# One decoder layer, 256 tokens, one core: the rotary queries and the middle norm's first columns transposed by 32x32 squares and transfers

## The chip, the cores and the metric

The kernel runs on one core of a Trainium2 chip. The metric is the time of one execution in device microseconds (us), the median of several runs; lower is better. TensorE (PE) does the matrix products and the 128x128 transposes, VectorE (DVE), ScalarE (ACT) and GpSimd (POOL) the elementwise work, SyncE (SP) issues most transfers (DMAs) between HBM and the on-chip memory.

## The reference

```
h  = x + 1/2 * SwiGLU_1(RMSNorm(x))                 # 1024 -> 2816 -> 1024
u  = RMSNorm(h)
[q_a,k_a,v_a | q_b,k_b,v_b | g_a,g_b] = u @ W_in    # 1024 -> 5120
y_a = block-sparse attention(rotary(q_a), rotary(k_a), v_a)   # 8 heads of 64; 256 tokens are one block
y_b = stick-breaking attention(q_b, k_b, v_b)                 # 8 heads of 64
m  = sigmoid(g_a) * (y_a @ W_branch_a) + sigmoid(g_b) * (y_b @ W_branch_b)   # 512 -> 1024, twice
h  = h + m @ W_out                                  # 1024 -> 1024
h  = h + 1/2 * SwiGLU_2(RMSNorm(h))
out = RMSNorm_final(h)                              # all float32, x is (1, 256, 1024)
```

## The kernel before

The 256 tokens are two halves t = 0, 1 of 128 partitions. Every weight matrix is cut into 376 tiles of 128x512 and laid in one stream in the order in which they are used. `Weights` loads the stream from HBM in chunks of two tiles (`raw`, 512 KB, issued by SP, three buffers), ACT rounds a tile to its high part `wh`, DVE forms the rest `wl`, and each product is three TensorE passes (`mm3`: wh with the high part of the left operand, wl with the high part, wh with the low part; 128x512 each). A *unit* is one such product of one tile and one t; after each unit the program's clock (`weave.tick`) goes on by one and tasks that are due are written into the program there: the delays D_... are counted in units. What stands in an engine's queue runs in that order.

A left operand must have its columns on the partitions, so it is transposed first. There are two ways. `Normed.half` transposes four 128x128 blocks on TensorE into PSUM (`tp_`), then splits them (ACT casts the high part, DVE subtracts). `Normed.moved` transposes 32x32 squares on DVE (one instruction for 128x512), moves the squares with 16 DMAs of 32 partitions from SBUF to SBUF (`exchange`), and splits what landed. Before the change `moved` serves the first 512 columns of the norms u (ahead of the input projection) and z (ahead of the second FFN), and `exchange` serves q and k of the stick-breaking heads; q and k of the rotary heads (`qa`, `ka`; 8 TensorE transposes each, tiles `qtpa`, `ktpa`, ended in qTha/qTla and kTha/kTla) and all four halves of the merged branches m (`tp_m`, `mh`, `ml`; t = 0, 1 and column halves c = 0, 1) go through TensorE.

Where the text speaks of them: input projection `in0`..`in9` (16 units each; `in0` is q of the rotary heads, `in1` its k); POOL rotates qa and ka (four small operations each, `rotate`) after its Newton steps for the scale r_u (`inv_rms`); branch products `ba` (y_a, tiles yah, yal) and `bb` (y_b, ybh, ybl); their gates (`gate`, sigmoids on ACT); `wo` is the product with W_out.

Of the kernel before, what the change touches and what calls it, by code (L numbers as in the profile page):

```python
# [17 lines left out]
P = 128  # L18
# [10 lines left out]
CH = 2  # L29
# [12 lines left out]
D_PIECE = 2  # L42
D_TURN = 10
D_READY = 7
D_NORM = 4
D_SQUARES = 3
D_EIGHT = 6
D_MERGE = 8
D_FIRST = (9, 10)
D_RMS0 = 4  # L50
D_RMS1 = 5
# [77 lines left out]
class Weights:  # L129
# [9 lines left out]
    def load(self, n, tiles=0):  # L139

        n = min(n, N_TILES // CH)
        while self.loaded < n * CH + tiles:
            c, j = divmod(self.loaded, CH)
            if j == 0:
                nm = f"raw{c}"
                self.raw[c] = self.early(nm) if c < 12 else self.pool.tile([P, CH * 512], F32, name=nm, tag="raw", bufs=3)
            step = 1 if c < 4 else CH
            s = slice(j * 512, (j + step) * 512)
            self.nc.sync.dma_start(self.raw[c][:, s], self.stream[c, :, s])
            self.loaded += step  # L150

    def split(self):
        i = self.ready
        self.load(i // CH + 1)
        raw = self.raw[i // CH][:, i % CH * 512:i % CH * 512 + 512]
        hi = self.pool.tile([P, 512], F32R, name=f"wh{i}", tag="wh", bufs=self.bufs)
        lo = self.pool.tile([P, 512], F32R, name=f"wl{i}", tag="wl", bufs=self.bufs)
        g = self.gain(i)
        if g is None:
            self.nc.scalar.copy(hi, raw)  # L160
            self.nc.vector.tensor_sub(lo, raw, hi.bitcast(F32))  # L161
        else:
            self.nc.scalar.activation(hi, raw, AF.Copy, scale=g)  # L163
            self.nc.vector.scalar_tensor_tensor(lo, raw, g, hi.bitcast(F32), op0=ALU.mult, op1=ALU.subtract)  # L164
        self.parts[i] = hi, lo
        self.ready += 1
        if i % CH == CH - 1:
            del self.raw[i // CH]
            self.load(i // CH + 1 + 3)

    def pump(self):
        if self.ready < min(self.freed + self.bufs, self.at + self.ahead, N_TILES):
# [16 lines left out]
def hybrid_layer_kernel(ctx, tc, x, xt, pos, g_final, bgate, wstream, out):  # L189
# [4 lines left out]
    ordered.enter_context(tc.manual_schedule())  # L194
    consts = ctx.enter_context(tc.tile_pool(name="consts", bufs=1))
    wpool = ctx.enter_context(tc.tile_pool(name="wpool", bufs=1))
    work = ctx.enter_context(tc.tile_pool(name="work", bufs=1))
    psum = ctx.enter_context(tc.tile_pool(name="psum", bufs=1, space=PSUM))

    def acc_bank(nm):  # L200
        return psum.tile([P, 512], F32, name=nm, tag="acc", bufs=3)
# [5 lines left out]
        return psum.tile([P, 1024], F32, name=nm, tag="pr", bufs=2)  # L207

    def big(nm, dt=F32R):
        return work.tile([P, 1024], dt, name=nm, tag="big", bufs=24)  # L210

    def wide(nm, w=768):
        return work.tile([P, w], F32, name=nm, tag="f", bufs=4)
# [82 lines left out]
    def unit(o, a, w, first, last):  # L296
        mm3(o, a[0], a[1], w, first, last)
        weave.tick()
        W.pump()
# [41 lines left out]
    class Normed:  # L341
# [12 lines left out]
            split(self.parts[0][:, s], self.parts[1][:, s], tp)  # L354
            self.there.add(c)

        def moved(self, c):

            s = slice(c * 512, c * 512 + 512)
            q = big(f"{self.nm}q{self.t}{c}", F32)  # L360
            nc.vector.transpose(slots(q[:, 0:512], 4), plain(h[self.t][:, s]))
            yield D_SQUARES
            yield from exchange(q[:, 512:1024], q[:, 0:512], 4, [nc.sync, nc.gpsimd], 1)
            yield D_EIGHT
            split(plain(self.parts[0][:, s]), plain(self.parts[1][:, s]), slots(q[:, 512:1024], 4))
            self.there.add(c)
# [8 lines left out]
    class Given(Normed):  # L375
# [15 lines left out]
        def blk(self, k):  # L391
            o = k % 4 * T + self.t * P
            return [q[:, o:o + P] for q in self.made[k // 4 * 2:k // 4 * 2 + 2]]

    def lagged(n, lag):

        for k in range(n + lag):
            if k < n:
                yield 0, k
            if k >= lag:  # L400
                yield 1, k - lag
# [4 lines left out]
    def slots(q, n):  # L406

        return q[:, 0:n * P].rearrange("p (g s w) -> p s g w", g=4, s=n)

    def plain(q):  # L410
        return q.rearrange("p (s g w) -> p s g w", g=4, w=32)

    def exchange(moved, squares, n, queues, gap):

        w = 32
        for m in range(16):
# [3 lines left out]
            if m % len(queues) == len(queues) - 1:  # L420
                yield gap


    def ffn(base, xn, nm, on_half, lag, last=False):

# [4 lines left out]
        def hidden(b, t, bank):  # L430
# [10 lines left out]
            nc.vector.transpose(dst, plain(sh[:, 256:512]))  # L441
            if t == 1 and (b % 2 or b == FB - 1):
                weave.add(turn_hidden(p, n), D_TURNED)

        def later(f, *args):
            f(*args)
            return
            yield

        def turn_hidden(p, n):  # L450
            moved = big(f"hm_{nm}{p}", F32)
# [173 lines left out]
    def next_norm(dst, nm):  # L625
        def on_half(t, c, piece=None):
            def go():
                dst[t].half(c)
                dst[t].rms()
                return  # L630
                yield

            if c == 0:
                dst[t] = Normed(t, nm)
                weave.begin(dst[t].moved(c))
            else:
                weave.add(go(), D_NORM)

        return on_half
# [31 lines left out]
    def heads(b0, nm, res, rotary, diagonal):  # L671


        for j, which in enumerate("qk"):
            src = {}
            squares = None if rotary else big(f"{which}s{nm}", F32)

            def evac(t, ps, j=j, which=which, src=src, squares=squares):
                dst = row512(f"{which}{nm}{t}")
                if j == 0:  # L680
                    if nm == "a":
                        nc.gpsimd.tensor_scalar(rq[t], un[t].r, 0.125, None, op0=ALU.mult)
                    nc.scalar.activation(dst, ps, AF.Copy, scale=rq[t])
                else:
                    nc.scalar.activation(dst, ps, AF.Copy, scale=un[t].r)
                if rotary:
                    rotate(dst, t)
                else:
                    nc.vector.transpose(slots(squares, 8)[:, t:t + 7:2], plain(dst))
                src[t] = dst  # L690

            def turn(which=which, src=src, squares=squares):
                if rotary:
                    tp = two_banks(f"{which}tp{nm}")
                else:
                    tp = big(f"{which}m{nm}", F32)
                    yield from exchange(tp, squares, 8, [nc.sync, nc.gpsimd], 1)
                    yield D_LANDED
                for pr in range(4 if rotary else 0):
                    for t in range(2):  # L700
                        nc.tensor.transpose(tp[:, pr * 256 + t * P:pr * 256 + (t + 1) * P], src[t][:, pr * P:(pr + 1) * P], ident)
                if which != diagonal:
                    parts = big(f"{which}Th{nm}"), big(f"{which}Tl{nm}")
                    for c in range(2):
                        s = slice(c * 512, c * 512 + 512)
                        if rotary:
                            split(parts[0][:, s], parts[1][:, s], tp[:, s])
                        else:
                            split(plain(parts[0][:, s]), plain(parts[1][:, s]), slots(tp, 8)[:, c * 4:c * 4 + 4])
                            yield D_PIECE  # L710
                    ready = [[q[:, pr * 256:(pr + 1) * 256] for q in parts] for pr in range(4)]
                else:
# [5 lines left out]
                            split(dst[0], dst[1], tp4[rows, c * 2:c * 2 + 2])  # L718
                            yield D_PIECE
                    ready = [[q[:, pr % 2 * 512:pr % 2 * 512 + 512] for q in res["bd"][pr // 2]] for pr in range(4)]  # L720
                yield D_READY if rotary else D_READY - D_PIECE
                res[which] = ready

            if which == diagonal:
# [4 lines left out]
                            q5 = q[half * HD:(half + 1) * HD].rearrange("p (c j t) -> p c j t", c=2, j=2)  # L729
                            nc.gpsimd.memset(q5[:, :, 1 - half, :].bitcast(F32), 0.0)  # L730
            project(b0 + j, evac)
            weave.add(turn(), D_TURN if rotary else D_TURNED)

        vs = big(f"vh{nm}"), big(f"vl{nm}")

# [159 lines left out]
    def yk(y, k, t):  # L895
        return [q[:, k * 256 + t * P:k * 256 + (t + 1) * P] for q in y]
# [1 line left out]
    def gate_half(br, t, c):  # L898
        return gates[br, t][:, c * 512:c * 512 + 512]

    for c in range(2):
        banks = {}
        for t, k in lagged(4, 2):
            if k == 0:
                banks[t] = acc_bank(f"ba{t}{c}")
            i = W_BR + c * 4 + k
            unit(banks[t], yk(ys["a"], k, t), W.get(i), k == 0, k == 3)
            if t == 1:
                W.done(i)
        if c == 0:  # L910
            weave.flush(long=True)
            with tc.issue_after(marks["exp"]):
                for br in range(2):
                    for t in range(2):
                        nc.scalar.activation(gates[br, t], gates[br, t], AF.Sigmoid)
        for t in range(2):
            nc.vector.tensor_mul(merged[t, c], banks[t], gate_half(0, t, c))

    mn = [None, None]

    def merge(t, c, ps):
        mb = wide(f"mb{t}{c}", 512)
        nc.vector.tensor_mul(mb, ps, gate_half(1, t, c))
        nc.vector.tensor_add(merged[t, c], merged[t, c], mb)

        def go():
            if mn[t] is None:
                mn[t] = Normed(t, "m")
            mn[t].half(c, merged[t, c])
            return  # L930
            yield

        weave.add(go(), D_MERGE)

    for t in range(2):
        for c in range(2):
            ps = acc_bank(f"bb{t}{c}")
            for k in range(4):
                i = W_BR + 8 + c * 4 + k
                unit(ps, yk(ys["b"], k, t), W.get(i), k == 0, k == 3)  # L940
                if t == 1:
                    W.done(i)
            merge(t, c, ps)


    zn = [None, None]
# [108 lines left out]
```

## Time and profile before

| | |
|---|---|
| median of 3 runs | 556.45 us (556.43 to 556.68) |
| the profiled execution | 555.9 us, of which the span 554.2 us and 1.7 us around it |
| TensorE busy | 546.1 us of the span (99%) |
| VectorE, ScalarE, GpSimd busy | 401.3, 338.1, 70.1 us |

The span runs from the first to the last instruction of the profiled execution; "busy" excludes the issuing of DMAs and waiting. The profiled execution is 0.55 us below the median.

### The profile page before, as it was taken

Reading aid. Unit: us, or ns where it says so; the run is one execution under the profiler, and the core shown is the slowest. Engines: PE = TensorE matmul, PEld = TensorE weight load, DVE = VectorE, ACT = ScalarE, POOL = GpSimd, SP = SyncE. Lnnn points to the kernel's source line nnn. Section 1 sums busy time; section 2 is a strip of 40 time slices with the busy share of each in tenths; the row PEclk is TensorE's granted clock in tenths of the full one; section 3 lists DMA queues with packets and bytes.
Section 4 is the critical chain, followed back from the end, with each engine's and each line's share of the span. In section 5 each row is a group of like instructions: output and inputs, shape, how many; then the busy total and the mean of one; then the engine's idle time right before and its main releaser. Section 6 shows DMA issues by size and latency. Waiting matters only on the chain.

```text
span 554.2 us, 7853 instructions
## 1 busy us (share of the span) xinstructions
PE 546.1 (99%) x2494; PEld 449.5 (81%) x2494; DVE 401.3 (72%) x694; ACT 338.1 (61%) x576; POOL 70.1 (13%) x141
## 2 busy tenths in 40 slices
PE   9999999999999999999999999999999999999995
PEld 5788888888888888888888888888888888888884
DVE  6887788766466676889888888777677678655645
ACT  6865656655454767677875774476556566544633
POOL 1200000000003746022022200460000000000000
PEclk9999999999999999999999999999999999999998
DMA  8946766775685677455545464576657766757722
GB/s 311 403 141 202 220 216 216 220 237 184 210 235 179 200 232 220 155 159 183 176 151 172 137 202 149 179 242 216 219 180 234 238 206 200 229 179 230 243 79 76
DMA packets 42937, 111.69 MB, mean 202 GB/s; under 512 B 8080, under 2 KB 16528, under 8 KB 42896
## 3 DMA queue, kind: packets, MB, share of 16 engines
q1 hardware_dynamic: 40464, 107.90, 60.9%
q0 software_dynamic: 2000, 2.62, 1.8%
q10 hardware_dynamic: 432, 0.67, 0.3%
q8 instruction: 19, 0.31, 0.3%
q14 instruction: 22, 0.18, 0.1%
HBM read 102.25 MB, written 1.05 MB: 186 GB/s over the span
## 4 chain that ended last, share of the span: by engine, by line
PE 95%; DMA 3%; ACT 0%; DVE 0%; issue 0%; ACTq 0%
PE gu_f L293 14%; PE gu_f L294 14%; PE gu_f L292 14%; PE dn_f L294 7%; PE dn_f L292 7%; PE dn_f L293 7%; PE in L292 7%; PE in L294 7%; PE in L293 7%; DMA raw<-in_wstream 2%; PE wo L294 1%; PE wo L292 1%; PE wo L293 1%; PE y_a L748 1%; PE z L748 1%; PE y_b L748 1%
## 5 line engine op out<-in xcount | busy, mean ns | idle before, releaser
L164 DVE SCALAR_TENSOR_TENSOR wl<-raw,first,wh 128x512 fp32r<-128x512 f32 x256 | 181.8, 747 | 41.3 <-ACT wh L163 40.1
L163 ACT ACTIVATE wh<-raw,first 128x512 fp32r<-128x512 f32 x256 | 171.7, 717 | 56.3 <-DMA raw<-in_wstream 31.0
L160 ACT CAST wh<-raw 128x512 fp32r<-128x512 f32 x120 | 70.4, 620 | 63.9 <-DMA raw<-in_wstream 40.8
L161 DVE TENSOR_TENSOR wl<-raw,wh 128x512 fp32r<-128x512 f32 x120 | 78.6, 691 | 40.0 <-ACT wh L160 39.9
L292 PE MATMUL gu_f<-wh,zh 128*128 128x512 f32 x176 | 68.6, 390 | 0.0
L294 PE MATMUL gu_f<-wh,zl 128*128 128x512 f32 x176 | 68.5, 389 | 0.0
L293 PE MATMUL gu_f<-wl,zh 128*128 128x512 f32 x176 | 68.5, 389 | 0.0
L292 PE MATMUL dn_f<-wh,hth_f 128*128 128x512 f32 x172 | 67.1, 390 | 0.0
L294 PE MATMUL dn_f<-wh,htl_f 128*128 128x512 f32 x172 | 66.9, 389 | 0.0
L293 PE MATMUL dn_f<-wl,hth_f 128*128 128x512 f32 x172 | 66.9, 389 | 0.0
L292 PE MATMUL in<-wh,uh 128*128 128x512 f32 x160 | 63.5, 397 | 0.0
L293 PE MATMUL gu_f<-wl,xh 128*128 128x512 f32 x160 | 62.4, 390 | 0.3 <-DVE wl L164 0.3
L294 PE MATMUL in<-wh,ul 128*128 128x512 f32 x160 | 62.5, 391 | 0.0
L292 PE MATMUL gu_f<-wh,xh 128*128 128x512 f32 x160 | 62.4, 390 | 0.1
L293 PE MATMUL in<-wl,uh 128*128 128x512 f32 x160 | 62.4, 390 | 0.0
L294 PE MATMUL gu_f<-wh,xl 128*128 128x512 f32 x160 | 62.2, 389 | 0.0
L293 PEld LDWEIGHTS gu_f<-wl,zh 128*128 128x128 f32 x176 | 33.0, 188 | 6.9
L294 PEld LDWEIGHTS gu_f<-wh,zl 128*128 128x128 f32 x176 | 33.0, 188 | 6.8
L292 PEld LDWEIGHTS gu_f<-wh,zh 128*128 128x128 f32 x176 | 33.0, 188 | 6.8
L292 PEld LDWEIGHTS dn_f<-wh,hth_f 128*128 128x128 f32 x172 | 32.3, 188 | 6.9 <-DVE sh_f L433 0.4
L294 PEld LDWEIGHTS dn_f<-wh,htl_f 128*128 128x128 f32 x172 | 32.3, 188 | 6.7
L293 PEld LDWEIGHTS dn_f<-wl,hth_f 128*128 128x128 f32 x172 | 32.3, 188 | 6.7
(247 smaller groups left out, 756.5 us busy)
## 6 DMA issues: line engine op xcount, KB each, us to landing
raw<-in_wstream SPq DMA_DIRECT2D x184, 512.0 KB, 4.3
hm_f<-hs_f SPq DMA_DIRECT2D x160, 32.0 KB, 4.2
raw<-in_wstream SPq DMA_DIRECT2D x8, 256.0 KB, 4.9
h<-in_x SPq DMA_DIRECT2D x2, 512.0 KB, 6.6
bg<-in_bgate POOLq DMA_DIRECT2D x4, 256.0 KB, 4.6
xin<-in_xt SPq DMA_DIRECT2D x3, 256.0 KB, 5.1
hm_f<-hs_f SPq DMA_DIRECT2D x32, 16.0 KB, 3.1
gB<-in_g_final POOLq DMA_DIRECT2D x1, 512.0 KB, 6.2
```

Of the source, the lines that this page charges most:

```text
L160: self.nc.scalar.copy(hi, raw)
L161: self.nc.vector.tensor_sub(lo, raw, hi.bitcast(F32))
L163: self.nc.scalar.activation(hi, raw, AF.Copy, scale=g)
L164: self.nc.vector.scalar_tensor_tensor(lo, raw, g, hi.bitcast(F32), op0=ALU.mult, op1=ALU.subtract)
L292: nc.tensor.matmul(o, ah, wh, start=first, stop=False)
L293: nc.tensor.matmul(o, ah, wl, start=False, stop=False)
L294: nc.tensor.matmul(o, al, wh, start=False, stop=last)
L748: nc.tensor.matmul(o, a[p], b[q], start=first and i == 0, stop=last and i == 2, skip_group_check=True)
```

## The change

- The rotary q: DVE transposes each half of `qa` by squares into `qsa` as soon as POOL has rotated it; one DMA on SP writes the 512 KB to a buffer in HBM (`there`), four DMAs of 128 KB read them back with the squares in place (`qma`), and the split reads `qma` instead of the PSUM tile. The 8 `qtpa` transposes go. k stays on TensorE.
- The middle norm m: columns c = 0 of both halves go by `moved` (tile `mq`), with 16 DMAs each: for t = 0 on SP, POOL and ACT in turn, for t = 1 on SP and POOL. Columns c = 1 stay on TensorE. 8 of 16 `tp_m` transposes go.
- The branch products run in the order ba c0, bb c0, ba c1, bb c1 (before: ba c0, ba c1, bb t0, bb t1), and the weight stream with them. The sigmoids are eight of 128x512 ahead of the first branch's weights (before: four of 128x1024 among them).
- Weight chunks have four buffers and are loaded one chunk earlier; the pool `big` has 23 tiles in place of 24.

```
+D_WRITTEN = 9
+D_ROTATED = 4
+D_SQUARED = 3
+D_MERGED = (3, 7)
-D_MERGE = 8
+D_MERGE = (4, 7)
...
-            self.load(i // CH + 1 + 3)
+            self.load(i // CH + 1 + (4 if i // CH >= 12 else 3))
...
+    def by_hbm(moved, squares, n):
+        w = n * 32
+        there = hbm.tile([P, 4 * w], F32, name="there")
+        nc.sync.dma_start(there, squares)
+        yield D_WRITTEN
+        for i in range(4):
+            nc.sync.dma_start(moved[:, i * w:(i + 1) * w],
+                              there[i * 32:i * 32 + 32, :].rearrange("r (j c) -> j r c", j=4))
...
                 if rotary:
                     rotate(dst, t)
+                    if j == 0:
+                        weave.add(later(square, t, dst), D_ROTATED)
...
-    for c in range(2):
+    def branch(nm, c, y, i0, make):
         banks = {}
-        for t, k in lagged(4, 2):
+        for t, k in lagged(4, 2 if nm == "ba" else 4):
...
+        if c == 0:
+            mn[t] = Normed(t, "m")
+            weave.begin(mn[t].moved(c, merged[t, c], D_MERGED[t], (nc.sync, nc.gpsimd, nc.scalar)[:3 - t]))
+        else:
+            weave.add(later(mn[t].half, c, merged[t, c]), D_MERGE[t])
...
+    for c in range(2):
+        branch("ba", c, ys["a"], W_BR + c * 8, first_part)
+        if c == 0:
+            weave.flush(long=True)
+        branch("bb", c, ys["b"], W_BR + c * 8 + 4, merge)
```

How the instructions stand, at the three places of which the prediction speaks. First VectorE's queue where `in0` gives way to `in1`; ul are the low parts of u for t = 1, v_u and r_u belong to its scale, wl are weight tiles in order of use. Before:

```order
L327 TENSOR_SCALAR v_u_2047<-v_u_2047 128x1
L328 TENSOR_SCALAR r_u_1882<-v_u_2047 128x1
L164 SCALAR_TENSOR_TENSOR wl_2034<-raw_1957,first,wh_2033 128x512
L314 TENSOR_TENSOR ul_1881<-uq_1883,uh_1880 128x512
L314 TENSOR_TENSOR ul_1881<-tp_u_2040,uh_1880 128x512
L164 SCALAR_TENSOR_TENSOR wl_2051<-raw_1957,first,wh_2050 128x512
L164 SCALAR_TENSOR_TENSOR wl_2094<-raw_1987,first,wh_2093 128x512
L164 SCALAR_TENSOR_TENSOR wl_2101<-raw_1987,first,wh_2100 128x512
```

and after the change:

```order
L332 TENSOR_SCALAR v_u_2052<-v_u_2052 128x1
L319 TENSOR_TENSOR ul_1885<-tp_u_2045,uh_1884 128x512
L319 TENSOR_TENSOR ul_1885<-uq_1887,uh_1884 128x512
L333 TENSOR_SCALAR r_u_1886<-v_u_2052 128x1
L695 STREAM_TRANSPOSE qsa<-qa_2082 128x4x4x32
L168 SCALAR_TENSOR_TENSOR wl_2099<-raw_1961,first,wh_2098 128x512
L168 SCALAR_TENSOR_TENSOR wl_2106<-raw_1961,first,wh_2105 128x512
```

The weight tile after the transpose is the same in both (wl_2094 before, wl_2099 after: the third tile of `in1`). The transpose stands ahead of it and reads what POOL rotates; and the start of the scale of t = 1 (r_u), for which POOL's Newton steps wait, has moved behind the two ul.

Second, VectorE's queue ahead of the first transposes of m on TensorE. Before, the last rows that they wait for are mb and m of t = 0 and c = 0, ahead of all weights of the next product:

```order
L161 TENSOR_TENSOR wl_3610<-raw_3549,wh_3609 128x512
L923 TENSOR_TENSOR mb_3615<-bb_3582,gate_0_3313 128x512
L924 TENSOR_TENSOR m_3467<-m_3467,mb_3615 128x512
L923 TENSOR_TENSOR mb_3631<-bb_3618,gate_0_3313 128x512
L924 TENSOR_TENSOR m_3468<-m_3468,mb_3631 128x512
L161 TENSOR_TENSOR wl_3642<-raw_3569,wh_3641 128x512
```

After, the first transposes on TensorE are those of t = 0 and c = 1 (m_3473):

```order
L366 STREAM_TRANSPOSE mq_3609<-m_3474 128x4x4x32
L165 TENSOR_TENSOR wl_3653<-raw_3519,wh_3652 128x512
L939 TENSOR_TENSOR m_3473<-ba_3611,gate_0_3021 128x512
L165 TENSOR_TENSOR wl_3680<-raw_3558,wh_3679 128x512
L165 TENSOR_TENSOR wl_3691<-raw_3558,wh_3690 128x512
L939 TENSOR_TENSOR m_3475<-ba_3644,gate_1_3032 128x512
L165 TENSOR_TENSOR wl_3702<-raw_3574,wh_3701 128x512
L165 TENSOR_TENSOR wl_3711<-raw_3574,wh_3710 128x512
L319 TENSOR_TENSOR ml_3580<-mq_3582,mh_3579 128x512
L943 TENSOR_TENSOR mb_3716<-bb_3673,gate_0_3318 128x512
L944 TENSOR_TENSOR m_3473<-m_3473,mb_3716 128x512
```

ml_3580, which needs all 16 transfers of `mq` for t = 0, stands ahead of the mb and m that the transposes read.

Third, ScalarE's and SyncE's queues at the same place, after the change. ScalarE:

```order
L164 CAST wh_3640<-raw_3519 128x512
L428 DMA mq_3582<-mq_3582 32x128 x5
L164 CAST wh_3652<-raw_3519 128x512
L164 CAST wh_3679<-raw_3558 128x512
```

SyncE (mq_3582 is t = 0):

```order
L153 DMA raw_3574<-in_wstream 128x1024
L428 DMA mq_3582<-mq_3582 32x128 x4
L153 DMA raw_3632<-in_wstream 128x1024
L428 DMA mq_3582<-mq_3582 32x128 x2
L153 DMA raw_3656<-in_wstream 128x1024
```

Five of the 16 transfers stand on ScalarE ahead of four weight casts, six on SyncE with a weight chunk among them; before, neither queue had any of them here. In the program the fifth on ScalarE and the chunk on SyncE each wait for an earlier small transfer of their own queue to have landed.

## Rows read from the trace of the kernel before

**Rows 1.** The page's parts on busy time and on 40 equal slices of the span (tenths; PEclk is the granted TensorE clock), and the chain that ended last by engine.

```profile
PE 546.1 (99%) x2494; PEld 449.5 (81%) x2494; DVE 401.3 (72%) x694; ACT 338.1 (61%) x576; POOL 70.1 (13%) x141
...
PEclk9999999999999999999999999999999999999998
...
PE 95%; DMA 3%; ACT 0%; DVE 0%; issue 0%; ACTq 0%
```

**Rows 2.** All waits of TensorE: us in total, times, longest.

```profile
PE warm L283 <- DVE zeros L262: 1.1, 1, 1.1
PE gu_f L293 <- DVE wl L164: 0.3, 1, 0.3
```

**Rows 3.** TensorE in order of time around the transposes of q: start, duration, what. Durations overlap; the start-to-start time is what one costs.

```profile
204.43 0.40 PE L294 MATMUL in<-wh,ul 128*128 128x512 f32 x1
204.67 1.04 PE L701 MATMUL qtpa<-ident,qa 128*128 128x128 f32 x8
205.46 0.47 PE L292 MATMUL in<-wh,uh 128*128 128x512 f32 x1
...
207.39 0.40 PE L294 MATMUL in<-wh,ul 128*128 128x512 f32 x1
```

**Rows 4.** The same around the first three groups of transposes of m.

```profile
340.13 0.39 PE L294 MATMUL bb<-wh,ybl 128*128 128x512 f32 x1
340.37 0.60 PE L353 MATMUL tp_m<-ident,m 128*128 128x128 f32 x4
...
343.35 0.39 PE L294 MATMUL bb<-wh,ybl 128*128 128x512 f32 x1
343.58 0.60 PE L353 MATMUL tp_m<-ident,m 128*128 128x128 f32 x4
...
346.53 0.39 PE L294 MATMUL wo<-wh,ml 128*128 128x512 f32 x1
```

**Rows 5.** VectorE in order of time where `in0` gives way to `in1`; in brackets idle time before and what ended it.

```profile
189.90 0.15 DVE L328 TENSOR_SCALAR r_u<-v_u 128x1 int32<-128x1 int32 x1
...
191.69 0.68 DVE L314 TENSOR_TENSOR ul<-tp_u,uh 128x512 fp32r<-128x512 f32 x1
192.30 0.74 DVE L164 SCALAR_TENSOR_TENSOR wl<-raw,first,wh 128x512 fp32r<-128x512 f32 x1
194.06 3.08 DVE L164 SCALAR_TENSOR_TENSOR wl<-raw,first,wh 128x512 fp32r<-128x512 f32 x4 [1.02 <-ACT wh L163]
```

**Rows 6.** GpSimd in the same stretch and in a later one: Newton steps for r_u of t = 1, scale of q, four operations of `rotate` on qa of t = 0; then two operations of the rotation of ka.

```profile
190.26 0.86 POOL L338 TENSOR_SCALAR v_u<-r_u,v_u 128x1 f32<-128x1 f32 x1
...
193.27 0.34 POOL L338 TENSOR_SCALAR v_u<-r_u,v_u 128x1 f32<-128x1 f32 x1
193.71 0.27 POOL L339 TENSOR_SCALAR r_u<-v_u,r_u 128x1 f32<-128x1 f32 x1
194.06 0.21 POOL L682 TENSOR_SCALAR rq<-r_u 128x1 f32<-128x1 f32 x1
194.23 0.90 POOL L666 TENSOR_TENSOR t_qa<-qa,cos 128x128 f32<-128x128 f32 x1
...
196.67 0.79 POOL L669 TENSOR_TENSOR qa<-t_qa,t_qa 128x128 f32<-128x128 f32 x1
...
212.43 0.32 POOL L668 TENSOR_TENSOR t_ka<-ka,sin 128x64 f32<-128x64 f32 x1
212.82 0.46 POOL L669 TENSOR_TENSOR ka<-t_ka,t_ka 128x128 f32<-128x128 f32 x1
```

**Rows 7.** TensorE in `in1`: the wl pass of its third weight tile.

```profile
199.45 0.39 PE L293 MATMUL in<-wl,uh 128*128 128x512 f32 x1
```

**Rows 8.** TensorE where the two rotary operands are first used, and ScalarE's second cast of kTha before it.

```profile
218.89 0.59 ACT L313 CAST kTha<-ktpa 128x512 fp32r<-128x512 f32 x1 [0.76 <-DVE kTla L314]
...
222.22 0.39 PE L776 MATMUL S<-kTha,qTha 64*128 64x256 f32 x2
```

**Rows 9.** DMA issues by line: count, KB each, median us from issue to landing.

```profile
raw<-in_wstream SPq DMA_DIRECT2D x184, 512.0 KB, 4.3
...
zq<-zq SPq DMA_DIRECT2D x16, 16.0 KB, 4.0
zq<-zq POOLq DMA_DIRECT2D x16, 16.0 KB, 3.2
```

**Rows 10.** VectorE in the branch products: the last ybl, a pair mb and m, three weight tiles.

```profile
327.69 0.43 DVE L314 TENSOR_TENSOR ybl<-y_b,ybh 64x256 fp32r<-64x256 f32 x1
...
335.12 0.69 DVE L923 TENSOR_TENSOR mb<-bb,gate 128x512 f32<-128x512 f32 x1 [0.81 <-PE bb L294]
335.85 0.69 DVE L924 TENSOR_TENSOR m<-m,mb 128x512 f32<-128x512 f32 x1
...
339.22 2.05 DVE L161 TENSOR_TENSOR wl<-raw,wh 128x512 fp32r<-128x512 f32 x3
```

**Rows 11.** The exchange of the norm z for t = 0: VectorE's transpose by squares, SyncE's and GpSimd's issues in order of time, ScalarE's wait for the last landing.

```profile
350.90 0.71 DVE L361 STREAM_TRANSPOSE zq<-h 128x512 f32<-128x512 f32 x1
...
351.70 0.51 SPq L418 DMA_DIRECT2D zq<-zq  x1
353.42 0.33 SPq L149 DMA_DIRECT2D raw<-in_wstream  x1
353.80 1.15 SPq L418 DMA_DIRECT2D zq<-zq  x2
355.04 0.53 SPq L149 DMA_DIRECT2D raw<-in_wstream  x1
355.61 3.05 SPq L418 DMA_DIRECT2D zq<-zq  x5
...
352.18 3.95 POOL L418 DMA_DIRECT2D zq<-zq  x8 [34.70 <-PE wo L294]
...
361.16 0.62 ACT L313 CAST zh<-zq 128x512 fp32r<-128x512 f32 x1 [2.79 <-DMA zq<-zq]
```

**Rows 12.** The times from issue to landing of all transfers of that exchange: least, median, most.

```profile
DMA to landing us min/median/max: 1.6/3.5/5.4
```

**Rows 13.** TensorE's first matmul after the two products of the first column half of `ba` (326.76) in order of time.

```profile
326.76 0.39 PE L292 MATMUL ba<-wh,yah 128*128 128x512 f32 x1
```

More of the change, by code (lines that the diff above doesn't have):

```diff
@@ L145, in load @@
                 nm = f"raw{c}"
-                self.raw[c] = self.early(nm) if c < 12 else self.pool.tile([P, CH * 512], F32, name=nm, tag="raw", bufs=3)
+                self.raw[c] = self.early(nm) if c < 12 else self.pool.tile([P, CH * 512], F32, name=nm, tag="raw", bufs=4)
             step = 1 if c < 4 else CH
@@ L196, in hybrid_layer_kernel @@
     wpool = ctx.enter_context(tc.tile_pool(name="wpool", bufs=1))
+    hbm = ctx.enter_context(tc.tile_pool(name="hbm", bufs=1, space=bass.MemoryType.DRAM))
     work = ctx.enter_context(tc.tile_pool(name="work", bufs=1))
@@ L209, in big @@
     def big(nm, dt=F32R):
-        return work.tile([P, 1024], dt, name=nm, tag="big", bufs=24)
+        return work.tile([P, 1024], dt, name=nm, tag="big", bufs=23)
     def wide(nm, w=768):
@@ L355, in half, with moved @@
             self.there.add(c)
-        def moved(self, c):
+        def moved(self, c, src, wait, queues=(nc.sync, nc.gpsimd)):
             s = slice(c * 512, c * 512 + 512)
             q = big(f"{self.nm}q{self.t}{c}", F32)
-            nc.vector.transpose(slots(q[:, 0:512], 4), plain(h[self.t][:, s]))
-            yield D_SQUARES
-            yield from exchange(q[:, 512:1024], q[:, 0:512], 4, [nc.sync, nc.gpsimd], 1)
+            nc.vector.transpose(slots(q[:, 0:512], 4), plain(src))
+            yield wait
+            yield from exchange(q[:, 512:1024], q[:, 0:512], 4, queues, 1)
             yield D_EIGHT
@@ L393, in blk, with later @@
             return [q[:, o:o + P] for q in self.made[k // 4 * 2:k // 4 * 2 + 2]]
+    def later(f, *args):
+        f(*args)
+        return
+        yield
     def lagged(n, lag):
@@ L443, in hidden @@
                 weave.add(turn_hidden(p, n), D_TURNED)
[L445 to L448, printed above, removed]
         def turn_hidden(p, n):
@@ L634, in on_half @@
                 dst[t] = Normed(t, nm)
-                weave.begin(dst[t].moved(c))
+                weave.begin(dst[t].moved(c, h[t][:, 0:512], D_SQUARES))
             else:
@@ L675, in heads, with square, evac @@
             src = {}
-            squares = None if rotary else big(f"{which}s{nm}", F32)
-            def evac(t, ps, j=j, which=which, src=src, squares=squares):
+            squares = None if rotary and j else big(f"{which}s{nm}", F32)
+            def square(t, src, squares=squares):
+                nc.vector.transpose(slots(squares, 8)[:, t:t + 7:2], plain(src))
+            def evac(t, ps, j=j, which=which, src=src, square=square):
                 dst = row512(f"{which}{nm}{t}")
@@ L687, in evac @@
                     rotate(dst, t)
+                    if j == 0:
+                        weave.add(later(square, t, dst), D_ROTATED)
                 else:
-                    nc.vector.transpose(slots(squares, 8)[:, t:t + 7:2], plain(dst))
+                    square(t, dst)
                 src[t] = dst
             def turn(which=which, src=src, squares=squares):
-                if rotary:
+                if squares is None:
                     tp = two_banks(f"{which}tp{nm}")
@@ L696, in turn @@
                     tp = big(f"{which}m{nm}", F32)
-                    yield from exchange(tp, squares, 8, [nc.sync, nc.gpsimd], 1)
+                    if rotary:
+                        yield from by_hbm(tp, squares, 8)
+                    else:
+                        yield from exchange(tp, squares, 8, [nc.sync, nc.gpsimd], 1)
                     yield D_LANDED
-                for pr in range(4 if rotary else 0):
+                for pr in range(4 if squares is None else 0):
                     for t in range(2):
@@ L705, in turn @@
                         s = slice(c * 512, c * 512 + 512)
-                        if rotary:
+                        if squares is None:
                             split(parts[0][:, s], parts[1][:, s], tp[:, s])
@@ L720, in turn @@
                     ready = [[q[:, pr % 2 * 512:pr % 2 * 512 + 512] for q in res["bd"][pr // 2]] for pr in range(4)]
-                yield D_READY if rotary else D_READY - D_PIECE
+                yield D_READY if squares is None else D_READY - D_PIECE
                 res[which] = ready
@@ L731, in heads @@
             project(b0 + j, evac)
-            weave.add(turn(), D_TURN if rotary else D_TURNED)
+            weave.add(turn(), D_TURN if squares is None else D_ROTATED + D_SQUARED if rotary else D_TURNED)
         vs = big(f"vh{nm}"), big(f"vl{nm}")
@@ L899, in gate_half, with first_part @@
         return gates[br, t][:, c * 512:c * 512 + 512]
-    for c in range(2):
+    mn = [None, None]
+    def branch(nm, c, y, i0, make):
         banks = {}
-        for t, k in lagged(4, 2):
+        for t, k in lagged(4, 2 if nm == "ba" else 4):
             if k == 0:
-                banks[t] = acc_bank(f"ba{t}{c}")
-            i = W_BR + c * 4 + k
-            unit(banks[t], yk(ys["a"], k, t), W.get(i), k == 0, k == 3)
+                banks[t] = acc_bank(f"{nm}{t}{c}")
+            unit(banks[t], yk(y, k, t), W.get(i0 + k), k == 0, k == 3)
             if t == 1:
[L909 to L919, printed above, removed]
+                W.done(i0 + k)
+            if k == 3:
+                make(t, c, banks[t])
+    def first_part(t, c, ps):
+        nc.vector.tensor_mul(merged[t, c], ps, gate_half(0, t, c))
     def merge(t, c, ps):
@@ L924, in merge @@
         nc.vector.tensor_add(merged[t, c], merged[t, c], mb)
[L926 to L943, printed above, removed]
+        if c == 0:
+            mn[t] = Normed(t, "m")
+            weave.begin(mn[t].moved(c, merged[t, c], D_MERGED[t], (nc.sync, nc.gpsimd, nc.scalar)[:3 - t]))
+        else:
+            weave.add(later(mn[t].half, c, merged[t, c]), D_MERGE[t])
+    assert all(("z", pr) in b for pr in range(4))
+    for c in range(2):
+        with tc.issue_after(marks["exp"]):
+            for br in range(2):
+                for t in range(2):
+                    nc.scalar.activation(gate_half(br, t, c), gate_half(br, t, c), AF.Sigmoid)
+    for c in range(2):
+        branch("ba", c, ys["a"], W_BR + c * 8, first_part)
+        if c == 0:
+            weave.flush(long=True)
+        branch("bb", c, ys["b"], W_BR + c * 8 + 4, merge)
     zn = [None, None]
@@ L1029 @@
     wa, wb, wo = (a[n][0] for n in ("w_branch_moba", "w_branch_sb", "w_out"))
-    for w in (wa, wb, wo):
-        st += tiles(w, 0, 512) + tiles(w, 512, 1024)
+    for ws in ((wa, wb), (wo,)):
+        for c in range(2):
+            for w in ws:
+                st += tiles(w, c * 512, c * 512 + 512)
     st += ffn_tiles(2)
```

## Prediction

> **What bounds the kernel now.** I read first the page's busy times and the chain that ended last [rows 1]: TensorE is busy 546.1 of 554.2 us, the chain is TensorE for 95% of the span, and the granted clock stands at its highest tenth in all slices but the last, so at the 2.4 GHz level. Then the waits [rows 2]: TensorE waited for another engine for 1.1 us while it warmed up and for 0.3 us once. There is therefore nothing to win by bringing data earlier. Only two things change the time: TensorE instructions that go, at the start-to-start time that they take, and new waits of TensorE, one to one. Last I read TensorE in order of time for the price of an instruction: 59 matmuls of 128x512 start between 326.76 [rows 13] and 340.13 [rows 4], which is 0.2266 us each, although each lasts 0.39 us.
>
> **What the change removes.** Around the q transposes, nine matmuls and eight transposes take from 204.43 to 207.39 [rows 3]: 2.96 less 9 x 0.2266 = 2.04 leaves 0.92 us for the eight. Around the first group of m, twelve matmuls and four transposes take from 340.13 to 343.35 [rows 4], 3.22 less 2.72 = 0.50; around the second, to 346.53, 3.18 less 2.72 = 0.46. The change takes away the eight and two of the four groups: 0.92 + 0.50 + 0.46 = **1.88 us**. Nothing is added on TensorE; the branch products are the same products in another order.
>
> **What it adds, place by place** (times on the clock of before; after the first gain of 0.92 both what is wanted and what delivers it come that much earlier).
>
> *The fourth weight buffer and the earlier loads.* They feed an engine that does not wait for weights [rows 2]. I take nothing.
>
> *The squares of q on VectorE, two of 0.71 us (as the one in [rows 11]).* The first stands ahead of the third weight tile of `in1` and reads what POOL rotates. Before, that tile's low part was begun at 194.06 [rows 5]; TensorE uses it at 199.45 [rows 7]. After, r_u comes behind both ul, which end at 192.37 [rows 5], so POOL starts at about 192.75, not 190.26 [rows 6]. POOL's durations come in two kinds in [rows 6]: 0.86, 0.90, 0.79 where VectorE works beside it, and 0.34, 0.27, 0.32, 0.46 where VectorE is mostly idle (it idles from 193.04 to 194.06 [rows 5]). While VectorE stands at the transpose it is idle. By the short rows three Newton steps and the scale take 3 x (0.44 + 0.35) + 0.21 = 2.6 us with their gaps, the rotation 0.46 + 0.32 + 0.32 + 0.46 = 1.6, so qa is ready at 196.9, the transpose ends at 197.6 and the tile at 198.4: 1.05 us to spare. By the long rows POOL takes the 7.2 us that it took before (190.26 to 197.46), qa is ready at 199.95 and the tile at 201.4: TensorE waits 1.95 us. I take the short rows, since VectorE does nothing in that time. The Trainium skill, page "SBUF — State Buffer", section "Who interferes with whom", states that a VectorE instruction with two SBUF inputs and a GpSimd one that reads SBUF block each other rather than share; by that rule the short rows hold here and the wait is nil, and the trace's short Newton rows in VectorE's idle time agree with it.
>
> *The detour of q through HBM.* The write can go out about when the transposes stood on TensorE, 204.7 [rows 3]. No row shows a write to HBM of this kind; the nearest is the read of a 512 KB chunk, 4.3 us [rows 9]. It lands at about 209.0, four reads at 0.6 us of issue each and 4.3 us land by 215.1, against a first use at 222.22 less 0.92 = 221.3 [rows 8]. Six us cover the casts and subtractions; SyncE's wait delays weight chunks, which the fourth buffer allows. ScalarE may stand at the cast of q until 215; kTha's second cast ended 2.7 us ahead of its use [rows 8], which is the cover left there. I take nothing, bounds 0 and 1 us.
>
> *The sigmoids ahead of the weights, the new order of the branches.* `bb` now begins at 326.76, in place of the second half of `ba` [rows 13], 5.4 us earlier than before (24 matmuls), and its fourth unit wants ybl, whose last piece ended at 328.12 [rows 10], at about 329.2. ScalarE's eight half sigmoids cost about what four whole ones did. One us is left; I take nothing, bounds 0 and 0.5.
>
> *The exchange of m for t = 0, and what stands behind it.* `bb` of t = 0 (twelve matmuls) ends at 326.76 + 2.72 = 329.5; mb, m and one weight tile at 0.72, 0.72 and 0.6 [rows 10] and the transpose end at about 332.9. Then 16 transfers go out, six by SyncE (0.6 us each, four, then a chunk that waits for a landing, then two), five by POOL, five by ScalarE. With landings of 2.3 to 3.5 us (between the least and the median, and the median, of [rows 12]), the chunk leaves at 335.3 to 336.5, the last two transfers by 336.5 to 337.7, and the last lands at L = 339.7 to 341.2. Behind it on VectorE stand ml (after its cast on ScalarE, 0.6), mb and m of t = 0, c = 1, which TensorE's first transposes read: L + 0.6 + 0.6 + 0.72 + 0.69 = L + 2.6 = 342.3 to 343.8. A second path leads to the same instruction: ScalarE's weight cast stands behind its five issues, the last of which waits for a landing, so that weight part comes at 336.7 to 338.2; then eight instructions at 0.61 and m at 0.72 make 342.3 to 343.8 as well. TensorE wants it where `ba` and `bb` of both halves are done up to four units of c = 1: at 343.05, by counting units from 326.76. The wait is 0 to 0.75 us; I take **0.4**, the middle. The exchange of t = 1 is wanted some 6 us later by the second product of `wo`; I take nothing.
>
> **Sum.** 1.88 - 0.4 = 1.5 us: the profiled execution goes from 555.9 (0.55 below its median) to 554.4, the median from 556.45 to **555.0**. A measurement of this kernel can tell some 0.2% from no change, 1.1 us, so this counts as faster, by little.
>
> **The rivals.**
>
> *Nothing waits.* Speaks for it that all covers above are positive at their short ends; against it that three of them are within 1 us. 556.45 - 1.88 = 554.6.
>
> *A wait eats the gain.* Two ways. POOL at its long rows makes TensorE wait 1.95 us at the third tile of `in1`: 556.45 - 1.88 + 1.95 = 556.5. Or the third queue buys nothing: the exchange of z, on two queues, took from 351.61 to 361.16, 9.55 us [rows 11]; at that pace L = 342.5, TensorE waits 2.05 us, and the time is 556.6. Against it: SyncE issued eight transfers there and two chunks, and issues six and one here. The Trainium skill, page "DMA: Bandwidth & Descriptors", section "Issuing engines are not separate DMA queues", says that several issuing engines only save the time to issue; by that rule two transfers and a chunk less on SyncE, some 1.8 us by its rows, are all that is won, and L would be near 340.7, within what I take.
>
> *Slower: the exchange lands late and holds VectorE's queue.* ml stands ahead of mb and m and of four more weight tiles, and the chunk on SyncE waits for a landing before the last two transfers go. At the longest landing of [rows 12], 5.4 us, the chunk leaves at 338.4, the last transfers by 340.1 and L = 345.5, TensorE waits 5.0 us and the time is 559.6. It decides from L = 343.4 on (wait 3.0 us, more than the gain and 1.1). Speaks for it that these transfers run beside weight chunks; against it the median of 3.5 us.
>
> **How the numbers follow.** Chances: the forecast, a small wait at the transposes of m, 0.35; nothing waits 0.25; the gain is eaten 0.28; slower 0.12. The range reaches from 554.4 (nothing waits, and a little for the error of the price) to 556.8 (the gain eaten); above it lies the slower case. The likeliest one's own range is 554.7 to 555.4. Faster by over 0.2% (below 555.3): most of the first two, 0.55. Within 0.2%: the gain eaten and the rest, 0.32. Slower: 0.13.
>
> **What would show it.** In the profile after: no `qtpa` rows, and eight `tp_m` in place of sixteen. Right if TensorE waits at `tp_m` of t = 0 for VectorE's m, by under 0.8 us, and nowhere else by over 0.3. The first step is wrong if it waits in `in1` for a weight part whose VectorE idled on POOL; then POOL's rotation rows are long. The exchange is sized wrong if ScalarE's cast of mh waits past 341.2 less 0.92. The price of a transpose is wrong if TensorE's busy time falls by something else than 1.9 us. What would make all of it wrong is a wait at a place that I gave a cover: the first product of the rotary heads, the fourth unit of `bb`, or weights late in the second FFN because SyncE's queue was held.

## The result, and the profile after

The changed kernel takes 563.6 us (562.17 to 564.09 over 4 runs) where the kernel before takes 556.5: 1.0123 times as long, 95% interval 1.0104 to 1.0141. It is 7 us slower, where 555.0 was forecast. The profiled execution took 563.6 us with a span of 561.9, 7.7 more than before.

The page of the changed kernel, the parts that answer to [rows 1]:

```profile
PE 548.1 (98%) x2478; PEld 449.8 (80%) x2478; DVE 403.6 (72%) x698; ACT 340.7 (61%) x580; POOL 71.6 (13%) x154
...
PEclk9999999999999999799999999999999999999999
...
PE 84%; DMA 6%; DVE 6%; issue 1%; ACT 1%; POOL 1%; ACTq 1%; SPq 0%; DVEq 0%; POOLq 0%
```

Two things are new: DMA and VectorE hold 6% of the chain each (before 3% and 0%), and in the seventeenth slice (225 to 239 us) the granted clock is below its level. TensorE has 16 instructions fewer, as counted, and is yet busy for longer. Its four longest waits, which answer to [rows 2]:

```profile
PE S L800 <- ACT kTha L318: 4.1, 1, 4.1
PE warm L288 <- DVE zeros L267: 1.1, 1, 1.1
PE tp_m L358 <- DVE m L944: 0.5, 1, 0.5
PE S L800 <- DVE kTla L319: 0.5, 1, 0.5
```

The wait at `tp_m` is the forecast one. The other new ones stand at the first product of the rotary heads, S. ScalarE's queue ahead of it, in order of time (idle time before in brackets):

```profile
222.60 1.14 ACT L318 CAST qTha<-qma 128x512 fp32r<-128x512 f32 x2 [9.45 <-DMA qma<-there]
223.64 1.94 ACT L167 ACTIVATE wh<-raw,first 128x512 fp32r<-128x512 f32 x3
225.49 0.56 ACT L318 CAST kTha<-ktpa 128x512 fp32r<-128x512 f32 x1
```

ScalarE stood 9.45 us at the cast of q, until the reads from HBM had landed; three weight casts and the cast of k, whose transposes had ended by 217.2, came behind. SyncE's side of it, the chain in order of time:

```profile
204.62 6.48 DMA there<-qsa
211.16 0.67 SPq L441
...
213.05 9.49 DMA qma<-there
```

The write took 6.5 us and not 4.3; the last read landed 9.5 us after its issue and not 4.3. What TensorE did then, in order of time:

```profile
221.61 0.39 PE L299 MATMUL in<-wh,ul 128*128 128x512 f32 x1
226.11 0.58 PE L800 MATMUL S<-kTha,qTha 64*128 64x256 f32 x2 [4.11 <-ACT kTha L318]
227.19 0.58 PE L800 MATMUL S<-kTla,qTha 64*128 64x256 f32 x2 [0.49 <-DVE kTla L319]
...
229.47 0.63 PE L299 MATMUL in<-wh,ul 128*128 128x512 f32 x1
229.89 0.63 PE L297 MATMUL in<-wh,uh 128*128 128x512 f32 x1
...
232.83 0.40 PE L298 MATMUL in<-wl,uh 128*128 128x512 f32 x1
233.06 0.40 PE L299 MATMUL in<-wh,ul 128*128 128x512 f32 x1
```

and the stretches around it (busy time of each engine, granted clock, DMA share, GB/s):

```profile
222.00:226.00 4.00, 0.00 (x0) 0.00 (x0) 2.75 (x5) 3.40 (x6) 0.00 (x0) 0.99 0.14 56
226.00:232.80 6.80, 6.20 (x22) 4.90 (x23) 6.14 (x10) 4.24 (x8) 0.00 (x0) 0.50 0.66 210
232.80:240.00 7.20, 7.20 (x36) 5.87 (x34) 5.29 (x13) 5.78 (x15) 0.00 (x0) 1.00 0.33 111
```

After 4.1 us without an instruction the granted clock fell to 0.50, the 1.2 GHz level, for 6.8 us: matmuls start 0.43 us apart, and 0.23 apart again from 232.8 on. By comparing the starts of the same instructions in both traces, the 7.7 us come about so: the first FFN 0.6 (in its first 18 us; the first experiment has the same code there and loses 0.1, and the kernel before with the fourth buffer alone loses 0.5 there in its profiled execution at an unchanged median, so this part varies between executions); the q transposes -0.9; the wait until S starts 4.2 (222.22 before, 226.11 now); the second wait and the half clock 3.5 (by 232.5 the difference stands at 7.4); a late low part at a product with the values (y_a) at 276 us 0.4; the branch products, m and the product with W_out -0.2.

### The profile page after: what moved, and what is told of

It is laid out like the page before. It is cut to its first block, busy times and chain, and to the rows that moved or that the text cites. A ratio compares the mean times of both kernels' runs of the same rounds, so it can differ in the third digit from the quotient of the medians.

```text
span 561.9 us, 7903 instructions
## 1 busy us (share of the span) xinstructions
PE 548.1 (98%) x2478; PEld 449.8 (80%) x2478; DVE 403.6 (72%) x698; ACT 340.7 (61%) x580; POOL 71.6 (13%) x154
## 4 chain that ended last, share of the span: by engine, by line
PE 84%; DMA 6%; DVE 6%; issue 1%; ACT 1%; POOL 1%; ACTq 1%; SPq 0%; DVEq 0%; POOLq 0%
PE gu_f L298 14%; PE gu_f L299 13%; PE gu_f L297 13%; PE dn_f L297 7%; PE dn_f L299 7%; PE dn_f L298 7%; PE in L297 5%; PE in L298 5%; PE in L299 4%; DMA raw<-in_wstream 2%; DVE wl L168 2%; DMA qma<-there 2%; DVE wl L165 1%; PE wo L297 1%; PE wo L299 1%; PE wo L298 1%
```

## The experiments

**The cause of the late reads.** In the changed kernel each read takes `there` by four column groups: its outermost dimension is 4. The trace between 212.5 and 216 us, when the reads run nearly alone (packets and their rate; the queue of SyncE and ScalarE, q1, and that of GpSimd, q0, with packets, MB and share of the 16 DMA engines' time; issues with time to landing):

```profile
DMA packets 303, 0.34 MB, mean 96 GB/s; under 512 B 8, under 2 KB 292, under 8 KB 303
...
q1 hardware_dynamic: 296, 0.31, 25.6%
q0 software_dynamic: 7, 0.03, 15.0%
...
raw<-in_wstream SPq DMA_DIRECT2D x2, 512.0 KB, 10.4
```

25.6% of 16 engines is the time of about four. By these rows a packet of q1 took 48 ns (25.6% of 16 x 3.5 us, over 296). Weight chunks issued behind the reads, from 213.7 on, took 10.4 us to land, not 4.3. Of the 303 packets only 11 have 2 KB or more, 7 of them on q0 and the other four from before 213.7: until 216 no engine took up the chunks that stood in the queue, not even those that the reads left idle. Why, no run shows.

The reads were late for a second reason as well. The packets from 212 to 223 us:

```profile
DMA packets 960, 2.05 MB, mean 186 GB/s; under 512 B 76, under 2 KB 588, under 8 KB 960
```

The 512 KB of the reads are the 512 packets between 512 B and 2 KB (588 less 76). From 212.5 to 216 there were 284 (292 less 8); the other 228 took until the cast at 222.5, beside weight chunks and gate biases. At the first pace they would have been there by about 219. That is an estimate from these counts; by it some 3 of the 9.5 us belong to what ran beside the narrow reads.

The first experiment cuts the same four reads by destination, 32 rows outermost:

```
-        for i in range(4):
-            nc.sync.dma_start(moved[:, i * w:(i + 1) * w],
-                              there[i * 32:i * 32 + 32, :].rearrange("r (j c) -> j r c", j=4))
+        for j in range(4):
+            nc.sync.dma_start(moved[j * 32:j * 32 + 32, :].rearrange("r (i c) -> r i c", i=4),
+                              there[:, j * w:(j + 1) * w].rearrange("(i r) c -> r i c", i=4))
```

> The changed kernel with one edit: the four reads of q from HBM are cut by destination (32 partitions each, 32 rows outermost) and not by source (four column groups outermost). Bytes, count, queue and time of issue stay. Theory A (each read as it was kept only about four of the 16 DMA engines busy, because its outermost dimension is 4): the reads land some 4 us after the last issue, by about 218 us, TensorE's wait of 4.1 us at the first S and the 6.8 us at half clock behind it go, and the time falls by about 7.4 us to 556.2 (555.4 to 557). Theory B (the reads are late because weight chunks and gate biases run beside them, or because they read what was just written): they land at about 222 again, TensorE waits about 4 us, 563 to 564.

It took 555.31 us, 0.9978 of before (0.9969 to 0.9987): 8.3 us less than the changed kernel, and 0.1 below the range that was expected. The reads' times to landing, ScalarE's cast of q, and TensorE's three longest waits:

```profile
DMA to landing us min/median/max: 4.5/4.9/5.1
```
```profile
216.46 1.13 ACT L318 CAST qTha<-qma 128x512 fp32r<-128x512 f32 x2
217.50 0.58 ACT L318 CAST kTha<-ktpa 128x512 fp32r<-128x512 f32 x1
```
```profile
PE warm L288 <- DVE zeros L267: 1.1, 1, 1.1
PE gu_f L310 <- DVE xl L319: 0.5, 1, 0.5
PE tp_m L358 <- DVE m L944: 0.4, 1, 0.4
```

ScalarE no longer waits at the cast, nor TensorE at S, and the page's clock row is that of before. Theory B, that neighbours or the just-written buffer alone make the reads slow, fails: the neighbours and the buffer are the same. It leaves open that neighbours lengthened the narrow reads, as estimated above. The slower write is not the cause either: it took 4.8 us here, but 6.1 and 6.2 in two later kernels with these wide reads (the low part of m later, three buffers), and TensorE does not wait at S there either. To see whether it is the outermost dimension that counts, the next goes the other way, eight reads with outermost dimension 2 and the 1 KB pieces unchanged:

```
+            for j in range(0, 4, 2):
+                nc.sync.dma_start(moved[j * 32:j * 32 + 64, i * w:(i + 1) * w],
+                                  there[i * 32:i * 32 + 32, j * w:(j + 2) * w].rearrange("r (j c) -> j r c", j=2))
```

> The changed kernel with each read of q from HBM cut in two (eight of 64 KB): outermost dimension of the source 2 in place of 4, the 1 KB pieces as they were. Theory A (the outermost dimension sets how many of the 16 DMA engines a read uses): in the stretch in which only these reads run, the engines' mean busy share falls from the 25.6% of the changed kernel to about 13%, at about half of its 96 GB/s; 512 KB at 48 GB/s take some 11 us from 211, so q lands at about 223 to 226, TensorE waits 4 to 8 us at the first S, 564 to 568. Rival (the pieces of 1 KB or the reading of just-written HBM are slow by themselves): the share stays near 25% or above, and the time at 563 to 564.

567.17 us (two runs), 1.0192 of before (1.0162 to 1.0221). DMA between 212.5 and 216 us (busy tenths of the 16 engines and GB/s in 40 slices; from the sixteenth on, gate biases run on q0 beside the reads), ScalarE's cast and TensorE's longest wait:

```profile
DMA  1111111111300009475777979999869983221143
GB/s 59 47 47 47 47 47 47 47 59 47 47 23 23 23 23 234 94 152 140 234 246 234 363 234 375 281 468 140 328 234 281 281 140 129 94 94 47 59 140 140
...
q1 hardware_dynamic: 159, 0.16, 13.6%
```
```profile
227.22 1.14 ACT L318 CAST qTha<-qma 128x512 fp32r<-128x512 f32 x2 [13.06 <-DMA qma<-there]
```
```profile
PE S L801 <- ACT kTha L318: 8.3, 1, 8.3
```

Half the rate (47 GB/s in place of 94 to 96), half the engines' time on q1 (13.6% in place of 25.6%), and twice the wait at S. A packet takes 48 ns as before (13.6% of 16 x 3.5 us, over 159), so the pieces have not become slower: fewer of them are under way at a time, and their number goes with the outermost dimension. The edit also halves the size of a read, and no run varies that alone; transfers of 32 KB with 32 rows outermost, in an experiment below, land in 3.3 to 5.7 us. The Trainium skill, page "DMA: Bandwidth & Descriptors", section "Why a DMA increments its semaphore by 16 and not by 1", has this rule: the number of engines is the largest up to 16 that divides the slowest dimension of both access patterns, and on the queues of SyncE and ScalarE they are the lowest-numbered ones. By it the reads as changed get 4 engines, all four reads the same 4, and those of this experiment 2; the 25.6%, the 13.6% and the halved rate agree. That chunks behind such reads stay off the other engines too, as the trace shows, does not follow from this rule.

**The parts apart.** The changed kernel with q back on TensorE:

```
-            squares = None if rotary and j else big(f"{which}s{nm}", F32)
+            squares = None if rotary else big(f"{which}s{nm}", F32)
...
-                    if j == 0:
-                        weave.add(later(square, t, dst), D_ROTATED)
```

> The changed kernel with q of the rotary heads back on TensorE (eight transposes, no squares, no HBM buffer); the middle norm, the branch order, the sigmoids and the fourth buffer as changed. Theory A and B alike: no wait at S, no half clock; against the changed kernel 7.4 us less and 0.9 us more for the transposes, 557.0; if the rest alone is worth what the prediction gave it (0.96 less 0.4), 555.9. Under 556.0 says the rest gains, over 556.9 that it loses (the 0.5 us lost in the first FFN and 0.4 us at a values product of the rotary heads would then belong to it).

556.04 us, 0.9993 of before (0.9984 to 1.0001), between the two marks that were set (556.0 and 556.9). The middle norm, the new order and the rest together are worth 0.4 us, not clear of zero by themselves; TensorE waits 0.4 us at `tp_m` there too. Against the first experiment, the detour of q with the wide reads gains 0.7 us, of the 0.92 that its transposes cost.

The squares of q moved from SBUF to SBUF, without HBM:

```
-                        yield from by_hbm(tp, squares, 8)
+                        yield from exchange(tp, squares, 8, [nc.sync, nc.gpsimd], 1)
```

> The changed kernel with the squares of q moved as those of the other heads are: 16 transfers of 32 KB from SBUF to SBUF on SyncE and GpSimd, no buffer in HBM. Theory A and B alike: each lands in about 4 us, all by 214 us, no wait at S, 556.2. If SyncE's and GpSimd's queues hold weights or the rotation of k up, TensorE waits at S or for a weight part and the time is above 557.

556.12 us, 0.9997 (0.9988 to 1.0006). The wait at S is gone here as well, but 0.8 us are lost between 263 and 269 us, where TensorE waits for low parts (vlb, pl) from VectorE. The first experiment has no loss there, but the changed kernel and the one with three buffers (below) lose 0.4 us at the same values product without this edit, so that it need not come from the 16 small transfers some 50 us earlier. What makes VectorE late there was not settled.

The fourth weight buffer alone, in the kernel before (the edit takes the pool `big` to 23 tiles as well):

```
-tag="raw", bufs=3)
+tag="raw", bufs=4)
-            self.load(i // CH + 1 + 3)
+            self.load(i // CH + 1 + (4 if i // CH >= 12 else 3))
```

> The kernel before with the fourth weight chunk buffer and the earlier loads alone. Expected: TensorE does not wait for weights in the kernel before, so no change, 556.4 (556.1 to 556.8). A rival: the earlier loads run beside the first FFN's own transfers and cost the 0.5 us that the changed kernel lost there, 557.

556.41 us, 1.0000 (0.9991 to 1.0009): nothing, as expected. And taken away from the kernel with the wide reads (those two lines reversed):

> The kernel with the reads cut by destination, with three weight chunk buffers and the loads of before. If the fourth buffer is what lets SyncE stand 1.7 us at the write of q and issue 16 small transfers of m among the chunks: weights come late behind one of the two, TensorE waits 0.5 to 2 us, 556 to 557.3. If three were enough: 555.3.

555.85 us (555.17 to 557.19), 0.9992 (0.9983 to 1.0001). The median is 0.5 us worse, and the runs lie farther apart than those with four buffers (554.77 to 555.63); the two intervals overlap, so a gain by the fourth buffer is not shown. In its profiled execution 0.5 us of the difference is in the first FFN and 0.4 us at a values product at 268 us, not behind the write or in the branch products: the places that I named are not where it loses. As both losses appear in kernels with four buffers too, they do not explain the median.

**The wait at the transposes of m.** In the kernel with the wide reads, VectorE, ScalarE's transfers and cast, and TensorE:

```profile
336.53 0.69 DVE L165 TENSOR_TENSOR wl<-raw,wh 128x512 fp32r<-128x512 f32 x1 [1.03 <-ACT wh L164]
...
340.75 0.69 DVE L319 TENSOR_TENSOR ml<-mq,mh 128x512 fp32r<-128x512 f32 x1
341.35 0.69 DVE L943 TENSOR_TENSOR mb<-bb,gate 128x512 f32<-128x512 f32 x1
342.07 0.69 DVE L944 TENSOR_TENSOR m<-m,mb 128x512 f32<-128x512 f32 x1
```
```profile
332.41 3.38 ACTq L428 DMA_DIRECT2D mq<-mq  x5
...
339.83 0.62 ACT L318 CAST mh<-mq 128x512 fp32r<-128x512 f32 x1 [1.24 <-DMA mq<-mq]
```
```profile
342.82 0.66 PE L358 MATMUL tp_m<-ident,m 128*128 128x128 f32 x4 [0.41 <-DVE m L944]
```

VectorE idles 1.03 us for the weight part behind ScalarE's five issues, and then runs without a gap until the m that TensorE reads. It is the second of the two paths of the prediction that decides, by little: the transfers have landed by 339.8, the cast of mh ends at 340.45, and ml starts at 340.75 without a wait for it. One edit puts ml behind that m:

```
-            yield D_EIGHT
-            split(...)
+            late = self.nm == "m" and self.t == 0
+            yield D_EIGHT + (4 if late else 0)
+            with tc.issue_after(marks["m01"]) if late else ExitStack():
+                split(...)
```

> The kernel with the reads cut by destination, and one more edit: on VectorE the low part of the exchanged m (t = 0, c = 0) comes behind the sum m of t = 0, c = 1 that TensorE's transposes read, not ahead of it. Theory A (TensorE's wait of 0.41 us at those transposes is VectorE's queue, in which 0.6 us of other work stands ahead): the wait goes, 555.31 - 0.4 = 554.9. Rival (the low part is wanted just as early by the third pass of the next product): the wait only moves there, 555.3.

554.58 us, 0.9968 of before (0.9955 to 0.9980): the wait is no longer in the list, and this kernel is 1.8 us faster than the one before. Its median is also 0.7 below that of the wide reads alone, but the two intervals overlap and the profiled executions take the same (554.85 and 554.77 us): the transposes start at 342.8 in both, because this execution gained some 0.3 us at them and had lost as much in the first FFN, where the code is the same. So the wait is shown to go, and the 0.7 us are not shown to come of it. All of TensorE's waits in it:

```profile
PE warm L288 <- DVE zeros L267: 1.1, 1, 1.1
PE gu_f L298 <- DVE v_x L332: 0.3, 1, 0.3
PE gu_f L310 <- ACT wh L167: 0.2, 1, 0.2
```

Last, the exchange of m for t = 0 without ScalarE (wide reads, ml where the change put it):

```
-            ... (nc.sync, nc.gpsimd, nc.scalar)[:3 - t]
+            ... (nc.sync, nc.gpsimd)
```

> The kernel with the reads cut by destination; the exchange of m for t = 0 goes on SyncE and GpSimd alone, eight transfers each, none on ScalarE. If the third queue only saves time of issue: two transfers and a chunk more on SyncE, the last landing some 1.8 us later than 339.8, so at about 341.6, the cast and the low part are then late for the first product of W_out, TensorE waits 0.5 to 1.5 us there, 555.8 to 556.5. If the third queue does not matter, or standing on ScalarE costs what it saves (the weight cast behind its five issues came 1.0 us late): 555.3 or 0.4 less.

555.46 us, 0.9983 (0.9974 to 0.9992), the same as with three queues (555.31). Its cast of mh and TensorE's wait:

```profile
342.82 0.62 ACT L318 CAST mh<-mq 128x512 fp32r<-128x512 f32 x1 [1.61 <-DMA mq<-mq]
```
```profile
PE wo L297 <- ACT mh L318: 0.5, 1, 0.5
```

The last landing is 3.0 us later (342.8 in place of 339.8), where 1.8 was expected. The wait at `tp_m` is gone, because ScalarE is free and ml now comes behind m on VectorE, and 0.5 us are waited at the product with W_out in its place.

## Why the prediction was wrong

- **The price of the transposes (1.88 us).** Right. In the changed kernel the difference falls by 0.92 us where the q transposes stood; with the wide reads TensorE is busy 544.1 us, 2.0 less than before. What the terms bring in time is a little less: some 0.7 us by q and 0.4 by the rest, against 0.92 and 0.96 less 0.4.
- **POOL at its short rows.** Right. In the changed kernel:

```profile
195.48 0.47 POOL L682 TENSOR_TENSOR t_qa<-qa,cos 128x128 f32<-128x128 f32 x1
...
196.59 0.46 POOL L685 TENSOR_TENSOR qa<-t_qa,t_qa 128x128 f32<-128x128 f32 x1
```
```profile
197.09 0.71 DVE L695 STREAM_TRANSPOSE qsa<-qa 128x512 f32<-128x512 f32 x1 [4.36 <-POOL qa L685]
197.72 5.24 DVE L168 SCALAR_TENSOR_TENSOR wl<-raw,first,wh 128x512 fp32r<-128x512 f32 x7
```

  qa ready at 197.05 (196.9 was worked out, [rows 6] has 197.46 for a start 2.5 us earlier), VectorE idle 4.36 us at the transpose, and no wait of TensorE for it.
- **The detour of q.** This step failed. It took the landing of a weight chunk, 4.3 us [rows 9], for the write and for the reads. The write needed 6.5 us, which the cover could bear: 6.1 and 6.2 us with the wide reads cost no wait. "Four reads at 0.6 us of issue each and 4.3 us land by 215.1" priced reads that have 4 rows outermost by a chunk that has 128; the last took 9.5 us, and they landed at 222.5. The bounds of 0 and 1 us were made around that one row, and the shape of the transfer, which stood in the diff, was not compared with the row's. The step named the cover (2.7 us behind kTha, ScalarE standing at the cast) but not its price when it is gone: 4.6 us of waits. On top of that came 6.8 us at half clock, some 3 us more: the opening premise, that new waits of TensorE cost their own length, "one to one", fell short for a wait of this length. The prediction did name the place among its signs of being wrong ("the first product of the rotary heads").
- **The sigmoids, the order of the branches, the weights.** TensorE did not wait there.
- **The wait at the transposes of m (0.4 us).** Right: 0.5 in the changed kernel, 0.4 with the wide reads, where ScalarE's issues, one of the two paths given, came last. One sum in it does not close: the terms given for the transpose of t = 0 end at 332.2 and not 332.9. With the wide reads it ended at 332.4, which is 333.2 on the clock of before, so the 0.7 us without a row came near by luck.
- **The rivals.** The slower one put the late exchange on m, at 559.6; a late exchange it was, but that of q, and the time lies beyond every rival. With that one step repaired the sum holds within 0.3 us: 555.0 forecast, 555.31 measured.

## What to carry to other kernels

Before a DMA gets the price of another row, compare the outermost dimension of both its sides, not only bytes and queue. In this kernel, with TensorE 99% busy, a late operand cost its wait, and a wait of several us cost some 3 us more in clock: so after 4.6 us of waits, and in the kernel with paired reads, 11.9 us slower than the one with wide reads at 8.7 us of waits. A task that waits for a transfer should not stand in a queue ahead of work that is ready: here a cast of q held the cast of k, and one low part moved behind the work that TensorE waited for took that wait away, in the kernel with the lowest median.

## What the runs showed of the hardware that was not expected

- A read with outermost dimension 4 ran at 96 GB/s in a quarter of the DMA engines' time (25.6%), one with 2 at 47 GB/s (13.6%), at 48 ns for a packet in both; the same 512 KB cut with 32 outermost landed in 4.5 to 5.1 us per read. Chunks queued behind the narrow reads needed 10.4 us, and none of their packets moved before 216, though issued from 213.7 on.
- After 4.1 us without a TensorE instruction the granted clock was 0.50 from 226.0 to 232.8, while TensorE worked nearly without a gap, and then 1.00 again.
- A third queue for 16 small transfers brought the last landing 3.0 us forward (342.8 to 339.8) and left the time as it was (555.46 and 555.31 us): five issues took ScalarE 3.38 us, and VectorE stood 1.03 us for the weight part behind them.
